# Turned w_up tiles of a hybrid decoder layer: one started per pair of row tiles in ScalarE's order, written whole to a place of their own two pairs later

## The chip, the cores and the metric

The kernel runs on one core of a Trainium2 chip. The metric is device microseconds of one execution, the median over several; lower is better. A core has TensorE (PE, matmuls into PSUM banks), VectorE (DVE), ScalarE (ACT), GpSimd (POOL) and SyncE (SP, which here issues nearly all DMAs). Each engine works through its own queue in order and waits at the head of it until what the instruction needs is there.

## The reference, cut to what matters

One decoder layer on 256 tokens of width 2048, all in float32. The change touches the last third, the MLP:

```python
def squared_relu_mlp(u, w_up, w_down):        # u 256 x 2048, w_up 2048 x 8192, w_down 8192 x 2048
    hdn = jax.nn.relu(jnp.einsum('bsd,df->bsf', u, w_up))
    return jnp.einsum('bsf,fd->bsd', hdn * hdn, w_down)

h = h + rmsnorm(mix, norm_mix_post)
h = h + rmsnorm(squared_relu_mlp(rmsnorm(h, norm_mlp_pre), w_up, w_down), norm_mlp_post)
```

## The kernel before

**Products.** Every weight tile (256 rows by 512 columns, 512 KB, two blocks of 128 rows) is fetched by SyncE into a place called `raw` and split in two fp32r parts: ScalarE writes `hi`, a rounded copy, and VectorE writes `lo` = raw - hi (`split`, L148 and L149). TensorE then forms a product from three matmuls: hi and lo with the rounded activations, hi with their remainder. There are five buffers each of hi and lo (`BUFS`), so ScalarE can be at most five tiles ahead of TensorE. A *row tile* is one weight tile with both halves of the tokens: 12 matmuls. A *pair of row tiles* is the same 256 weight rows for two neighbouring column blocks: 24 matmuls.

**Sevens.** For some rows k a pair of row tiles is done as one step of Strassen's scheme (`seven`): seven products (21 matmuls) in place of eight, with sums of weights made by VectorE (`e`, `r`, L261) and sums of activations (`sums_of_acts`, L400 to L405). Half of the second weight tile then comes as a sum made by GpSimd in DRAM (`pair`). `plan` lists for each unit the order of the rows and which of them are sevens.

**Units.** `unit` computes 256 tokens by two column blocks (1024 columns) over all rows. It accumulates in eight PSUM banks, `acc` (four) and `more` (four). After the last seven, `combine` (`combine_new`, L450 to L454) empties the four banks of `more` on ScalarE and VectorE; after the last pair, `at_end` empties `acc`. The next unit swaps the two: its first pair of row tiles writes where `more` was. The MLP goes in two halves `hf` of 4096 features: the units of w_up for 8 column blocks (7 units in all are planned so), then two units of w_down over those 4096 features, then the same again.

**Turned tiles.** A unit of w_up leaves four tiles of 128 tokens by 512 features, in `room["shared"]` (tiles `hb` and `wpost`). w_down needs them with the features on the partitions. `up_end` (L1470) adds the last bank (L1475), applies Relu on ScalarE (L1476) with high priority, and queues `turned` (L1480) in `beside`: Square (L1483), the 16-bit halves of each word put apart by a ScalarE copy into a place of halves (L1484), a DMA transpose back into the tile (L1485, on SyncE's queue), and some steps later the halves put together by a second ScalarE copy (L1490) into the same place of halves, and a split into the activations of w_down. `pump_beside` moves the oldest of these works one step on: once per row tile in w_up (`pace` 1, `lag` 2), twice in w_down (2 and 3), twice per seven. `drain_beside` finishes them all before `combine`, and in the first unit of each w_down before its first seven (`more_beside_down`, `more_in_place`), since the places of halves lie in `ha`, which then becomes the place for sums of activations or for weights.

**What sets the order.** The instructions of `weights` and `seven` carry a very high priority and are chained in the order of the program (`split_in_line`, `add_in_line`); the rest is put between them by a list scheduler. Weight tiles go round a ring of places: four in `raw`, and those in `room["raw"]`, which stage by stage are tiles that nothing else uses then (`mw0`, `mw1`, `mw2`, `ha`, `uc`). SyncE's queue holds fetches and transposes in one order, and a fetch waits there until its place is free.

## Time and profile before

| | |
|---|---|
| runs, median (lowest to highest) | 1463.38 us (1462.07 to 1464.75) |
| the profiled execution, its own time | 1466.13 us |
| its span, first to last instruction | 1464.0 us |
| TensorE busy in the span | 1438.5 us, 98% |
| VectorE, ScalarE busy | 1297.8 us, 89%; 999.0 us, 68% |
| granted TensorE clock, mean | 0.993 |
| TensorE, VectorE, ScalarE busy from 840 to 1440 us | 582.77, 551.22, 433.01 us of 600 |

The MLP's part that the change touches begins at about 850 us (the first turned tile is copied apart at 853.3 us) and ends with the kernel. Busy TensorE time counts pipelined matmuls: in an undisturbed stretch one begins every 0.227 us and is listed with 0.39 us.

### The profile page before, as it was taken

How to read it: one execution, taken by the hardware profiler on the slowest of the kernel's cores; microseconds unless marked ns; L12 is line 12 of the kernel's file. 1: busy time of each engine (PE TensorE's matmuls, PEld its weight loads, DVE VectorE, ACT ScalarE, POOL GpSimd, SP SyncE). 2: the span in 40 equal slices, each digit the busy share in tenths (PEclk: the TensorE clock that was granted, in tenths of full speed). 3: DMA queues.
4: the chain of work that ended last, by engine and by line, in shares of the span. 5: the costliest groups of instructions: out<-in, count | busy, mean ns of one | idle time of the engine just before them, and what ended most of it. 6: DMA issues, size and time to landing. Idle time of an engine off the chain costs nothing.

```text
span 1464.0 us, 20242 instructions
## 1 busy us (share of the span) xinstructions
PE 1438.5 (98%) x6930; PEld 1204.8 (82%) x6930; DVE 1297.8 (89%) x1881; ACT 999.0 (68%) x1407; POOL 162.7 (11%) x244
## 2 busy tenths in 40 slices
PE   9999999999999999999999999989999999989998
PEld 8888888888888888888888888867888887768886
DVE  7788888988999788699989999879889999969998
ACT  7577669675666666566667689855565888876564
POOL 0201110121101000010100111001111011101000
PEclk9999999999999999999999999989999999999999
DMA  8967666756888657588877799688888999989854
GB/s 267 280 204 222 188 186 182 236 173 187 245 256 240 190 130 243 204 246 268 266 215 228 236 314 286 195 192 237 271 253 247 260 273 270 271 211 305 261 197 164
DMA packets 201926, 340.30 MB, mean 232 GB/s; under 512 B 45616, under 2 KB 48544, under 8 KB 201824
## 3 DMA queue, kind: packets, MB, share of 16 engines
q1 hardware_dynamic: 174304, 279.72, 61.3%
q0 software_dynamic: 19648, 45.63, 15.4%
q10 hardware_dynamic: 7872, 13.68, 2.8%
q8 instruction: 54, 0.88, 0.2%
q14 instruction: 48, 0.39, 0.1%
HBM read 327.39 MB, written 49.84 MB: 258 GB/s over the span
## 4 chain that ended last, share of the span: by engine, by line
PE 61%; DVE 7%; ACT 4%; DMA 3%; issue 2%; SPq 0%; ACTq 0%; DVEq 0%
PE acc L355 8%; PE acc L353 8%; PE acc L354 8%; PE acc L442 5%; PE acc L443 5%; PE acc L441 5%; PE acc L510 4%; DVE lo L149 4%; PE acc L513 2%; PE ps L443 2%; PE ps L442 2%; PE ps L441 2%; PE ps L353 2%; PE ps L354 2%; PE ps L355 2%
## 5 line engine op out<-in xcount | busy, mean ns | idle before, releaser
L149 DVE TENSOR_TENSOR lo<-raw,hi 128x1024 fp32r<-128x1024 f32 (+1 forms) x402 | 487.1, 1218 | 79.1 <-ACT hi L148 76.8
L148 ACT ACTIVATE hi<-raw 128x1024 fp32r<-128x1024 f32 (+1 forms) x402 | 419.0, 1049 | 191.9 <-PE acc L355 50.0
L510 PE MATMUL acc<-ua,hi 128*128 128x512 f32 x520 | 141.2, 400 | 0.0
L148 ACT ACTIVATE hi<-e 128x1024 fp32r<-128x1024 f32 x66 | 69.7, 1057 | 49.3 <-DVE e L261 45.3
L510 PEld LDWEIGHTS acc<-ua,hi 128*128 128x128 f32 x520 | 91.3, 189 | 14.0
L353 PE MATMUL acc<-hi,ua 128*128 128x512 f32 x228 | 90.0, 395 | 0.0
L149 DVE TENSOR_TENSOR lo<-e,hi 128x1024 fp32r<-128x1024 f32 x66 | 80.5, 1220 | 10.3 <-ACT hi L148 9.9
L354 PE MATMUL acc<-lo,ua 128*128 128x512 f32 x228 | 89.2, 391 | 0.0
L355 PE MATMUL acc<-hi,ua 128*128 128x512 f32 x228 | 89.0, 390 | 0.0
L353 PE MATMUL acc<-hi,sh 128*128 128x512 f32 x220 | 86.4, 393 | 0.0
L355 PE MATMUL acc<-hi,sl 128*128 128x512 f32 x220 | 85.7, 389 | 0.0
L354 PE MATMUL acc<-lo,sh 128*128 128x512 f32 x220 | 85.6, 389 | 0.0
L513 PEld LDWEIGHTS acc<-ua,lo 128*128 128x128 f32 x520 | 76.5, 189 | 8.9
L513 PE MATMUL acc<-ua,lo 128*128 128x256 f32 x520 | 78.8, 281 | 0.0
L442 PE MATMUL acc<-lo,ah 128*128 128x512 f32 x180 | 70.6, 392 | 1.8 <-DVE lo L149 1.7
L441 PE MATMUL acc<-hi,ah 128*128 128x512 f32 x180 | 70.2, 390 | 0.6 <-ACT hi L148 0.6
L443 PE MATMUL acc<-hi,al 128*128 128x512 f32 x180 | 70.1, 389 | 0.0
L510 PE MATMUL acc<-uc,hi 128*128 128x512 f32 x208 | 61.4, 405 | 0.0
L443 PE MATMUL acc<-hi,ua 128*128 128x512 f32 x137 | 53.3, 389 | 0.0
L442 PE MATMUL acc<-lo,ua 128*128 128x512 f32 x137 | 53.3, 389 | 0.0
L441 PE MATMUL acc<-hi,ua 128*128 128x512 f32 x137 | 53.0, 390 | 0.0
L355 PEld LDWEIGHTS acc<-hi,ua 128*128 128x128 f32 x228 | 42.8, 188 | 9.0
(566 smaller groups left out, 3714.4 us busy)
## 6 DMA issues: line engine op xcount, KB each, us to landing
raw<-in_w_in_dram SPq DMA_DIRECT2D x154, 512.0 KB, 4.4
raw<-in_w_up_dram SPq DMA_DIRECT2D x77, 512.0 KB, 4.8
raw<-in_w_down_dram SPq DMA_DIRECT2D x70, 512.0 KB, 5.7
raw<-in_w_out_dram SPq DMA_DIRECT2D x38, 512.0 KB, 5.0
raw<-pair SPq DMA_DIRECT2D x59, 256.0 KB, 4.5
pair<-in_w_up_dram POOLq DMA_DIRECT2D x56, 256.0 KB, 6.3
pair<-in_w_down_dram POOLq DMA_DIRECT2D x52, 256.0 KB, 6.5
pair<-in_w_in_dram POOLq DMA_DIRECT2D x42, 256.0 KB, 5.4
```

Of the source, the lines that this page charges most:

```text
L148: return (nc.scalar.activation(hi, src, AF.Copy), nc.vector.tensor_tensor(lo, src, hi.bitcast(F32), op=ALU.subtract))
L149: nc.vector.tensor_tensor(lo, src, hi.bitcast(F32), op=ALU.subtract))
L353: nc.tensor.matmul(dst[:, cs], a_h[:, r, ts], hi[:, j, cs], start=begin and j == 0, stop=False)
L354: nc.tensor.matmul(dst[:, cs], a_h[:, r, ts], lo[:, j, cs], start=False, stop=False)
L355: product[t] = nc.tensor.matmul(dst[:, cs], a_l[:, r, ts], hi[:, j, cs], start=False, stop=end and j == KB - 1)
L441: nc.tensor.matmul(dst, a_h, hi[:, j], start=own and first, stop=False)
L442: nc.tensor.matmul(dst, a_h, lo[:, j], start=False, stop=False)
L443: nc.tensor.matmul(dst, a_l, hi[:, j], start=False, stop=own and last)
L510: nc.tensor.matmul(acc[f], hi[:, j, f * P:(f + 1) * P], u(k0 + j), start=k0 + j == 0, stop=False, skip_group_check=True)
L513: nc.tensor.matmul(acc[f][:, 0], lo[:, j, f * P:(f + 1) * P], u(k0 + j)[:, 0], start=False, stop=k0 + j == NK - 1, skip_group_check=True)
```

## The change

Six things move together.

1. A tile is started by `pump_beside` once per row k (a pair of row tiles or a seven) from the third row on, and each start is tied into ScalarE's order right behind the newest split (`newest["act"]`). Relu moves from `up_end` into `turned`.
2. It is finished by `land_beside` at the end of the second row after that, tied in the same way.
3. The halves are put together into `whole`, a tile named `junk` of its own (one buffer), and not into the place of halves.
4. There are two places of halves, used in turn, in place of four: `mw1` in the first half of the MLP, a third of `ha` in the second.
5. So in the first half `ha` gives three places for weights (before: one) and `mw1` none; in the second half two (before: one). `beside_down` takes `ha` for sums at once, and the second half's w_down uses two thirds of `ha` for weights from its start; the rest follows as `then`, when the last tile has landed.
6. In the first unit of each w_down the rows are in another order: the first seven is the fourth row there, before the fifth, and the sevens then alternate with other rows.

```diff
-    def beside_up(raws, turn):
+    def beside_up(raws, turn, halves=None):
...
-        room["halves"] = [a[:, i].bitcast(U16) for i in range(2 * NT)]
-        room["raw"], room["turn"], room["acts"], room["chain"] = [*raws, a[:, 2 * NT:]], turn, act_u, True
-        room["pace"], room["lag"] = 1, 2
+        in_a = [a[:, k:k + KB] for k in range(0, 3 * KB, KB)]
+        halves = in_a.pop(0) if halves is None else halves
+        room["halves"] = deque(halves[:, i].bitcast(U16) for i in range(KB))
+        room["raw"], room["turn"], room["acts"], room["chain"] = [*raws, *in_a], turn, act_u, True
+        room["of_halves"], room["of_a"] = halves, in_a
...
+    def pump_beside():
+
+        if not beside:
+            return
+        work = beside.popleft()
+        with tc.issue_after(newest["act"].ins):
+            next(work)
+        flying.append([work, 0])
+
+    def land_beside(steps=2):
+
+        for one in flying:
+            one[1] += 1
+        if flying and flying[0][1] > steps:
+            with tc.issue_after(newest["act"].ins):
+                next(flying.popleft()[0], None)
+        if not (beside or flying) and "then" in room:
+            room.pop("then")()
...
-            plan(("down", 0), w_down, 0, (0, 1, 2, 3, 4, 5, 6, 7, 9, 8, 10, 11, 12, 13), (4, 6, 9, 10, 11, 13))
+            plan(("down", 0), w_down, 0, (0,1,2,4,3,6,5,9,7,10,8,11,12,13), (4,6,9,10,11,13))
...
         for i, (k, by_seven) in enumerate(order):
+            if i >= 2:
+                pump_beside()
...
-                pump_beside(2)
...
+            land_beside()
...
-                nc.scalar.activation(r, r, AF.Relu, scale=rmlp[:, t:t + 1])
-            beside.append(turned(t, 4 * fb, r, room["halves"][NT * b + t]))
+            beside.append(turned(t, 4 * fb, r))
...
+        nc.scalar.activation(r, r, AF.Relu, scale=rmlp[:, t:t + 1])
         nc.scalar.activation(r, r, AF.Square)
...
-        steps = 0
-        while steps < room["lag"]:
-            steps += 1
-            yield
-        nc.scalar.activation(halves.rearrange("p (n h) -> p h n", h=2), words.rearrange("p (h n) -> p h n", h=2), AF.Copy)
+        yield
+        whole = hp.tile([P, NB], F32, name="junk")
+        nc.scalar.activation(whole.bitcast(U16).rearrange("p (n h) -> p h n", h=2), words.rearrange("p (h n) -> p h n", h=2), AF.Copy)
...
-        split(d_h[:, i:i + 4, ts], d_l[:, i:i + 4, ts], halves.bitcast(F32).rearrange("p (f s) -> p f s", f=4))
+        split(d_h[:, i:i + 4, ts], d_l[:, i:i + 4, ts], whole.rearrange("p (f s) -> p f s", f=4))
...
     in_u = room["raw"]
-    room["chain"], room["pace"], room["lag"] = True, 2, 3
+    room["raw"] = [*in_u, *room["of_a"]]
+    room["chain"] = True
```

The new text is 18 lines longer in all, so a line has another number after the change: Relu, Square and the first copy stand in L1500 to L1502, the transpose in L1503, the second copy in L1506, `up_end`'s addition in L1491, and `combine_new` in L464 to L468.

**First place: ScalarE where the first half of the MLP passes from w_up to w_down.** `hi` from `ha`, `raw` and `mw2` are the splits of weight tiles, `hb` and `wpost` the tiles of the unit of w_up that has just ended, `ha` (before) and `mw1` (after) the places of halves. Before:

```order
L1476 ACTIVATE hb_7889<-hb_7889,rmlp_5921 128x512 x2
L1483 ACTIVATE hb_7889<-hb_7889 128x512 x2
L1476 ACTIVATE wpost_7890<-wpost_7890,rmlp_5921 128x512
L1476 ACTIVATE wpost_7891<-wpost_7891,rmlp_5921 128x512
L148 ACTIVATE hi_9193<-mw2_6211 128x1024
L1484 ACTIVATE ha_7892<-hb_7889 128x1024
L148 ACTIVATE hi_9214<-raw_9212 128x1024
L1484 ACTIVATE ha_7892<-hb_7889 128x1024
L148 ACTIVATE hi_9243<-raw_9241 128x1024
L1483 ACTIVATE wpost_7890<-wpost_7890 128x512
L1483 ACTIVATE wpost_7891<-wpost_7891 128x512
L1484 ACTIVATE ha_7892<-wpost_7890 128x1024
```

and now, from the second copy of the third tile of the unit before on:

```order
L1506 ACTIVATE junk_9055<-wpost_7890 128x2x512
L148 ACTIVATE hi_9110<-raw_9108 128x1024
L148 ACTIVATE hi_9128<-raw_9126 128x1024
L148 ACTIVATE hi_9146<-raw_9144 128x1024
L148 ACTIVATE ah0_4884<-junk_9055 128x4x128
L148 ACTIVATE hi_9164<-raw_9162 128x1024
L1500 ACTIVATE hb_7889<-hb_7889,rmlp_5921 128x512
L1501 ACTIVATE hb_7889<-hb_7889 128x512
L1502 ACTIVATE mw1_6210<-hb_7889 128x1024
L148 ACTIVATE hi_9193<-mw2_6211 128x1024
L148 ACTIVATE hi_9211<-raw_9209 128x1024
L1506 ACTIVATE junk_9059<-wpost_7891 128x2x512
```

The four Relus in a row are gone and one tile at a time stands between the splits; the second copies of the unit before (L1506) now stand behind the first splits of w_down (a Relu of the second tile, L1500, stands ahead of the last row).

**Second place: VectorE at the same point.** `acc_8016` is the fourth bank of `more`, which the second row tile of w_down writes next; `lo` from `raw` are the splits of w_down's first tiles. Before:

```order
L452 TENSOR_TENSOR hb_7889<-acc_8016,r_9057 128x512
L453 TENSOR_TENSOR wpost_7890<-acc_8014,r_9057 128x512
L1475 TENSOR_TENSOR hb_7889<-acc_8009,hb_7889 128x512
L454 TENSOR_TENSOR wpost_7891<-acc_8016,wpost_7890 128x512
L1475 TENSOR_TENSOR hb_7889<-acc_8011,hb_7889 128x512
L149 TENSOR_TENSOR lo_9138<-raw_9135,hi_9137 128x1024
```

and now:

```order
L149 TENSOR_TENSOR lo_9129<-raw_9126,hi_9128 128x1024
L149 TENSOR_TENSOR lo_9147<-raw_9144,hi_9146 128x1024
L149 TENSOR_TENSOR lo_9165<-raw_9162,hi_9164 128x1024
L415 TENSOR_TENSOR r_9185<-r_9184 128x256
L149 TENSOR_TENSOR lo_9194<-mw2_6211,hi_9193 128x1024
L416 TENSOR_TENSOR r_9185<-r_9184,r_9185 128x128
L149 TENSOR_TENSOR al0_4885<-junk_9055,ah0_4884 128x4x128
L417 TENSOR_TENSOR r_9185<-r_9184,r_9185 128x128
L149 TENSOR_TENSOR lo_9212<-raw_9209,hi_9211 128x1024
L468 TENSOR_TENSOR wpost_7891<-acc_8016,wpost_7890 128x512
```

The last instruction of `combine` (L454, now L468) writes `wpost_7891`, which L1506 reads; so it has moved behind that copy, behind six splits of w_down's tiles.

**Third place: SyncE where the second half passes to w_down.** `uc` and `ha` are places for weights, `hb` and `wpost` the tiles that are turned. Before:

```order
L162 DMA uc_12045<-in_w_down_dram 128x2x512
L157 DMA uc_12045<-pair4_93 128x512
L158 DMA uc_12045<-in_w_down_dram 128x512
L1485 DMA_TRANSPOSE hb_10525<-ha_10528 128x8x128 x2
L1485 DMA_TRANSPOSE wpost_10526<-ha_10528 128x8x128
L1485 DMA_TRANSPOSE wpost_10527<-ha_10528 128x8x128
L162 DMA ha_12216<-in_w_down_dram 128x2x512 x3
```

and now:

```order
L158 DMA raw_12378<-in_w_down_dram 128x512
L1503 DMA_TRANSPOSE hb_10533<-ha_10536 128x8x128 x2
L162 DMA uc_12047<-in_w_down_dram 128x2x512 x2
L1503 DMA_TRANSPOSE wpost_10534<-ha_10536 128x8x128
L162 DMA ha_10536<-in_w_down_dram 128x2x512
L157 DMA ha_10536<-pair2_91 128x512
```

Weight fetches into `ha` stood behind all four transposes; now two of its places are used before the first transpose is issued (a row `ha_10536<-in_w_down_dram` stands ahead of the rows shown, too), and the transposes stand one by one between fetches.

More of the change, by code (lines that the diff above doesn't have):

```diff
@@ L199, in beside_up @@
         a = hp.tile([P, 3 * KB, NB], F32, name="ha")
[L200 to L202 removed]
+        in_a = [a[:, k:k + KB] for k in range(0, 3 * KB, KB)]
[3 more added lines that the diff above has]
+        room["of_halves"], room["of_a"] = halves, in_a
         sums_of.clear()
     def beside_down():
[L207 to L210 removed]
+        a = hp.tile([P, 3 * KB, 2, S], F32R, name="ha")
+        room["sums"] = [a[:, k] for k in range(3 * KB)]
+        room["raw"], room["turn"], room["acts"], room["then"] = [mws[2]], 0, part, more_beside_down
         sums_of.clear()
     def more_beside_down():
[L215 to L216 removed]
         b = hp.tile([P, KB, 2, S], F32R, name="hb")
[L218 removed]
+        room["sums"] += [b[:, k] for k in range(KB)]
         room["sums"] += [hp.tile([P, 2, S], F32R, name="wpost", bufs=2) for _ in range(2)]
+        m = new_mw(1, F32R)
+        room["sums"] += [m[:, t].rearrange("p (b s) -> p b s", b=2) for t in range(NT)]
     def fetch_next(src, k0, c0, pair=None):
@@ L242, in hymba_layer @@
     behind = []
-    line = {}
+    line, newest = {}, {}
     @contextmanager
@@ L316, in weights @@
                     order.enter_context(tc.issue_after(behind.pop().ins))
-                split(hi, lo, raw)
+                newest["act"] = split(hi, lo, raw)[0]
         return hi, lo
@@ L332, in drain @@
             pump()
-    beside = deque()
-    def pump_beside(n=1):
-        for _ in range(n):
-            if beside:
-                work = beside.popleft()
-                if next(work, work) is not work:
-                    beside.append(work)
+    beside, flying = deque(), deque()
+    def pump_beside():
[13 more added lines that the diff above has]
+            room.pop("then")()
     def drain_beside():
-        while beside:
+        while beside or flying:
             pump_beside()
+            land_beside(0)
     def row_tile(dst, t, parts, k0, acts, begin, end, cs=slice(0, NB)):
@@ L377, in row_tiles @@
             pump(pumps)
-            pump_beside(room.get("pace", 1))
     def gemm_tokens(src, c0, acts, nk, lag=0, at_end=None, pumps=1):
@@ L1537, in hymba_layer @@
     in_u = room["raw"]
-    room["chain"], room["pace"], room["lag"] = True, 2, 3
+    room["raw"] = [*in_u, *room["of_a"]]
+    room["chain"] = True
     def more_in_place():
-        drain_beside()
-        a, b = hp.tile([P, 3 * KB, NB], F32, name="ha"), hp.tile([P, KB, 2, S], F32R, name="hb")
-        room["raw"] = [*in_u, *(a[:, k:k + KB] for k in range(0, 3 * KB, KB))]
+        b = hp.tile([P, KB, 2, S], F32R, name="hb")
         room["sums"] += [b[:, k] for k in range(KB)]
+        room["turn"] %= RAWS + len(room["raw"])
+        room["raw"].append(room["of_halves"])
         for n in range(2):
             load_wpost(norm_mlp_post, n)
+    room["then"] = more_in_place
     unit(w_downs[1], 0, orders[("down", 1), 0], (14, 15), acc, more,
-         lambda x: combine_onto(0, x), 0, (complete(0), complete(1)), ready=more_in_place)
+         lambda x: combine_onto(0, x), 0, (complete(0), complete(1)))
     room["chain"] = False
```

18 lines of the change are left out of this document (7 added, 11 removed).

## The prediction

> **What bounds the kernel now.** TensorE is busy for 98% of the span, and no matmul is added or removed, so a gain can only come from TensorE's own waits. I read first who waits for whom, TensorE alone, from 840 us on (total, times, longest).
>
> ```profile
> PE ps L353 <- ACT hi L148: 6.9, 1, 6.9
> PE acc L441 <- ACT hi L148: 6.7, 3, 5.4
> PE acc L442 <- DVE lo L149: 3.1, 6, 0.8
> PE ps L1433 <- ACT dg L1432: 1.4, 1, 1.4
> PE ps L354 <- DVE lo L149: 0.4, 2, 0.2
> ```
>
> Two waits hold most of it. L1433 is the kernel's end, which the change leaves alone. The timeline of TensorE (start, duration, in brackets the idle time before and who ended it) shows where the others lie and what follows them.
>
> ```profile
> 958.70 0.39 PE L441 MATMUL acc<-hi,mw 128*128 128x512 f32 x1
> 959.72 0.50 PE L442 MATMUL acc<-lo,mw 128*128 128x512 f32 x1 [0.63 <-DVE lo L149]
> 966.51 0.80 PE L441 MATMUL acc<-hi,mw 128*128 128x512 f32 x1 [5.36 <-ACT hi L148]
> 967.77 0.80 PE L442 MATMUL acc<-lo,mw 128*128 128x512 f32 x1 [0.46 <-DVE lo L149]
> 972.74 0.40 PE L355 MATMUL ps<-hi,sl 128*128 128x512 f32 x1
> ...
> 1202.72 0.50 PE L442 MATMUL acc<-lo,ah 128*128 128x512 f32 x1 [0.49 <-DVE lo L149]
> 1244.77 0.50 PE L441 MATMUL acc<-hi,ah 128*128 128x512 f32 x1 [0.64 <-ACT hi L148]
> 1246.03 0.50 PE L442 MATMUL acc<-lo,ah 128*128 128x512 f32 x1 [0.76 <-DVE lo L149]
> 1275.07 0.39 PE L353 MATMUL acc<-hi,uc 128*128 128x512 f32 x1
> 1280.51 0.39 PE L353 MATMUL ps<-hi,sh 128*128 128x512 f32 x1
> 1306.90 0.39 PE L443 MATMUL ps<-hi,sl 128*128 128x512 f32 x1
> 1314.16 1.22 PE L353 MATMUL ps<-hi,sh 128*128 128x512 f32 x2 [6.87 <-ACT hi L148]
> 1318.05 0.40 PE L353 MATMUL ps<-hi,sh 128*128 128x512 f32 x1
> ```
>
> From 1275.07 to 1280.51 stand the 24 matmuls of one pair of row tiles: 0.227 us each. At the first passage from w_up to w_down, 958.70 to 972.74, 17 matmuls take 14.04 us in place of 3.86: 10.2 us lost, of which some 3 are slow matmuls (0.63 to 0.80 us) after the long wait. At the second, 1306.90 to 1318.05, 11 matmuls take 11.15 in place of 2.50: 8.6 us. The other waits are 6.7 - 5.4 + 3.1 - 0.63 - 0.46 + 0.4 - 0.2 = 3.5 us, 1.9 of them in the second w_up (the rows at 1202 to 1246). **In all 22.3 us can go.**
>
> Next, who made the two long waits: ScalarE's and SyncE's timelines.
>
> ```profile
> 942.61 1.04 ACT L1484 ACTIVATE ha<-hb 128x1024 uint16<-128x1024 uint16 x1
> 956.13 1.37 ACT L1490 ACTIVATE ha<-hb 128x1024 uint16<-128x1024 uint16 x1 [4.29 <-DMA hb<-ha]
> 964.21 1.34 ACT L1490 ACTIVATE ha<-wpost 128x1024 uint16<-128x1024 uint16 x1 [4.05 <-DMA wpost<-ha]
> 965.43 1.03 ACT L148 ACTIVATE hi<-mw 128x1024 fp32r<-128x1024 f32 x1
> 1303.94 1.36 ACT L1490 ACTIVATE ha<-wpost 128x1024 uint16<-128x1024 uint16 x1
> 1313.05 1.06 ACT L148 ACTIVATE hi<-ha 128x1024 fp32r<-128x1024 f32 x1 [6.75 <-DMA ha<-in_w_down_dram]
> ```
>
> ```profile
> 945.88 2.27 SPq L162 DMA_DIRECT2D raw<-in_w_down_dram  x2
> 948.21 6.74 SPq L1485 DMA_TRANSPOSE hb<-ha  x2
> 958.22 5.00 SPq L1485 DMA_TRANSPOSE wpost<-ha  x1
> 1307.13 1.41 SPq L162 DMA_DIRECT2D ha<-in_w_down_dram  x3
> ```
>
> First passage: the first tile's halves are ready at 943.65, its transpose leaves SyncE only at 948.21 behind fetches, and the second copies (L1490) wait at the head of ScalarE, with the split at 965.43, for which TensorE waits, behind them. Second passage: the next places for weights are in `ha`, which holds halves until the last L1490 at 1303.94 and its split are through; the fetch leaves at 1307.13 and lands at 1313.
>
> **The change, step by step.** Per turned tile (28 of them) ScalarE still does Relu, Square, two copies and a split, SyncE one transpose, VectorE one split: nothing added, nothing saved. `whole` costs what L1490 does, being the same shape. The first passage's long wait needs an L1490 whose transpose is late; now each tile is landed two rows after its start, where some 12 to 15 us of other ScalarE work lie between, and transposes land as follows (group, count, median to landing, 920 to 960 us):
>
> ```profile
> raw<-in_w_down_dram SPq DMA_DIRECT2D x11, 512.0 KB, 5.4
> mw<-in_w_down_dram SPq DMA_DIRECT2D x1, 512.0 KB, 8.4
> hb<-ha SPq DMA_TRANSPOSE x2, 7.5
> wpost<-ha SPq DMA_TRANSPOSE x2, 8.3
> ```
>
> So that wait goes; if SyncE holds a transpose 5 us (958.22), cover is still there. The second long wait goes too: two thirds of `ha` hold no halves, and the fetches into them stand ahead of the first transpose. That transpose stands behind many fetches and is about 7 us late for its L1506, but TensorE then has five buffered tiles, some 7 us, in hand; I cost it at nothing, and at its 4 us of waiting (964.21) if the cover were gone.
>
> **What is late next** is the last instruction of `combine`, L454, now L468. It frees the fourth bank of `more`, overwrites `wpost_7891`, and now has to wait for L1506 of the unit before, which stands behind w_down's first splits on ScalarE; VectorE's queue stands behind it, and TensorE needs the bank. The rows for it:
>
> ```profile
> 1275.24 0.68 DVE L451 TENSOR_TENSOR r<-hb,ps 128x512 f32<-128x512 f32 x1
> 1278.77 0.68 DVE L454 TENSOR_TENSOR wpost<-acc,wpost 128x512 f32<-128x512 f32 x1
> ...
> L149 DVE TENSOR_TENSOR lo<-raw,hi 128x1024 fp32r<-128x1024 f32 x155 | 187.8, 1220 | 12.9 <-ACT hi L148 12.2
> L148 ACT ACTIVATE hi<-raw 128x1024 fp32r<-128x1024 f32 x155 | 162.0, 1053 | 62.3 <-PE acc L355 21.2 <-DMA raw<-in_w_down_dram 21.0 <-DMA raw<-in_w_up_dram 9.2
> L1490 ACT ACTIVATE ha<-wpost 128x1024 uint16<-128x1024 uint16 x14 | 19.0, 1358 | 4.4 <-DMA wpost<-ha 4.4
> ```
>
> Count from the last pair of w_up (0 = 1275.07 at the second passage). Before, VectorE begins `combine` at 0.2 and ends L454 at 4.4. TensorE comes to the bank at 5.4 + 18 x 0.227 = 9.5; the new order puts 11 matmuls (first passage) or 5 (second) of the next tile ahead: 12.0 and 10.6.
> - First passage. VectorE frees the place of w_down's first tile after five additions of 0.6 and a `lo`: 4.3. The fetch into it takes 5.4, then come a split 1.05, a Relu 0.6, L1506 1.36: 12.7, L468 ends 13.4. TensorE waits 1.4 us. By a landing of 8.4 it is 4.4; by VectorE's own row of work alone L468 ends at 12.9 and by ScalarE's buffers at 11.9, so nothing is the other end.
> - Second passage. 4.3 + 5.4 + 1.05 + 1.36 = 12.1, another 0.1 behind VectorE's own work, L468 ends 12.9: TensorE waits 2.2 us, by a landing of 8.4 5.2, by buffers alone nothing.
> - Three passages from unit to unit inside w_up: L468 stands behind eight additions, three `lo` and one L1506, and ends at 9.1 with the bank due at 9.5. I take 0.3 us each, 0.9, between 0 and 1.2 each (a transpose held 5 us).
>
> The waits in w_up (1.9 us) I let go: they follow clumps of Relus that are spread now, and a ring of five places that has six. Of the others 1.4 us stay, because VectorE is full there (busy us by engine in two stretches after the passages):
>
> ```profile
> 970.00:1020.00 50.00, 48.78 (x204) 38.16 (x203) 49.50 (x67) 31.92 (x37) 5.45 (x8) 0.97 0.79 227
> 1320.00:1370.00 50.00, 49.31 (x218) 40.40 (x217) 49.96 (x70) 32.19 (x37) 6.78 (x10) 1.00 0.92 282
> ```
>
> The third busy time is VectorE's: 49.5 and 49.96 of 50 us. The order of rows moves a seven earlier there and changes no sum; the alternation keeps VectorE's work even. I cost it at nothing, between -1 and 3 us.
>
> **Sum.** Left are 1.4 + 2.2 + 0.9 + 1.4 = 5.9 us of 22.3: 16.4 us gained. The profiled execution took 1466.13 us, so 1449.7; that one is 2.75 us above the runs' median, so against them **1447 us**.
>
> Whether such a wait also slows the matmuls behind it, the rows show from both sides: 0.76 us did not (0.50 us, then the usual pace), 5.36 us did, for some 3 us lost. My waits lie between, nearer the short one, so I add nothing. [...]
>
> **Rivals.**
> - *The bank waits take their far end.* For: landings of 8.4 us are in the trace, and L468 depends on one at both passages. Against: the median is 5.4. Then 4.4 + 5.2 with 3 us of slow matmuls each, 15.6 in place of 3.6: 1459 us.
> - *VectorE becomes the bound.* For: the stretches above. Its work between 920 and 1020 us must now fit in 10 us less, and every wait at L468 idles it. Against: the long ScalarE waits idled it before. Another 2 to 3 us at each passage: 1452 us.
> - *It doesn't do what it says*: second copies still wait at ScalarE's head, at 4 us for each of two late transposes at both passages, 16 us back: 1463 us. Against: the cover of 12 us.
> - *Slower.* One `junk` and L468 tie transpose, ScalarE, VectorE and bank in a ring at five passages. If the fourth tile's transpose lands later than about 12 us after its copy, L468 ends after 9.5 at each of them. At 5 us and 3 us of slow matmuls: 5 x 8 = 40 us in place of 4.5: 1482 us. Against: 8.3 us is the landing seen.
>
> **How the numbers follow.** Forecast 0.55 (1442 to 1452), far bank waits 0.18, VectorE 0.13, not as said 0.06, slower 0.08. A measurement of this kernel tells some 0.2%, 3 us, from no change. Faster: the first three, 0.86; same 0.06; slower 0.08. The range goes from 1439, all 22.3 us gone and the short matmul gaps behind each wait with them, to 1460, the far bank waits.
>
> **What would show it.** Right: no idle time before the second copies (L1506) that passes to TensorE, no `ha` wait of 6.75 us, and TensorE's longest wait after 850 us a matmul on the fourth bank of `more`, released by VectorE's L468, at 1 to 5 us, twice. Wrong: waits of that kind at the passages inside w_up, a clock below full there, or L1506 waiting for transposes longer than 4 us.

## The result and the profile after

| | before | changed |
|---|---|---|
| runs, median (lowest to highest) | 1462.72 us (1460.11 to 1464.75) | 1447.99 us (1446.84 to 1449.47) |
| the profiled execution's span | 1464.0 us | 1446.6 us |
| granted TensorE clock, mean | 0.993 | 0.999 |

The ratio is 0.9901 (95% interval 0.9882 to 0.992): 1% faster, 14.7 us between these medians and 17.4 us between the two profiled spans (the profiled execution of the kernel before took 1466.13 us, 3.4 us more than the median here). The forecast was 1447.0 us.

Who waits for whom in the changed kernel, TensorE alone, from 840 us on (total, times, longest):

```profile
PE acc L368 <- DVE wpost L468: 3.4, 3, 2.0
PE ps L1449 <- ACT dg L1448: 1.4, 1, 1.4
PE ps L369 <- DVE lo L149: 1.2, 2, 0.7
PE acc L456 <- DVE lo L149: 0.9, 2, 0.7
```

Without the kernel's end (L1449) 5.5 us of waits are left, of 17.1 before. Both long ones on ScalarE are gone, and the largest is now the fourth bank of `more`, released by VectorE's L468. TensorE's timeline says where:

```profile
943.42 0.50 PE L368 MATMUL acc<-hi,sh 128*128 128x512 f32 x1 [1.05 <-DVE wpost L468]
1189.72 0.50 PE L368 MATMUL acc<-hi,ua 128*128 128x512 f32 x1 [0.38 <-DVE wpost L468]
1275.55 0.50 PE L368 MATMUL acc<-hi,sh 128*128 128x512 f32 x1 [1.99 <-DVE wpost L468]
```

1.05 us at the first passage, 0.38 inside w_up, 1.99 at the second passage. ScalarE and VectorE at the first passage show how L468 comes to be late:

```profile
929.47 1.36 ACT L1506 ACTIVATE junk<-wpost 128x1024 uint16<-128x1024 uint16 x1
941.27 1.37 ACT L1506 ACTIVATE junk<-wpost 128x1024 uint16<-128x1024 uint16 x1 [0.99 <-DVE al L149]
```

```profile
935.48 3.48 DVE L149 TENSOR_TENSOR lo<-raw,hi 128x1024 fp32r<-128x1024 f32 x3
938.88 0.41 DVE L415 TENSOR_TENSOR r<-r 128x256 f32<-128x256 f32 x1
939.22 1.21 DVE L149 TENSOR_TENSOR lo<-mw,hi 128x1024 fp32r<-128x1024 f32 x1
940.35 0.28 DVE L416 TENSOR_TENSOR r<-r 128x128 f32<-128x128 f32 x1
940.56 0.68 DVE L149 TENSOR_TENSOR al<-junk,ah 128x512 fp32r<-128x512 f32 x1
941.16 0.28 DVE L417 TENSOR_TENSOR r<-r 128x128 f32<-128x128 f32 x1
941.36 1.21 DVE L149 TENSOR_TENSOR lo<-raw,hi 128x1024 fp32r<-128x1024 f32 x1
942.67 0.69 DVE L468 TENSOR_TENSOR wpost<-acc,wpost 128x512 f32<-128x512 f32 x1
```

The last tile's second copy (941.27) waits for the one buffer of `junk`, which VectorE empties at 940.56, in the middle of a row of work without a pause. No fetch is waited for. At the second passage one is:

```profile
1265.81 1.06 ACT L148 ACTIVATE hi<-raw 128x1024 fp32r<-128x1024 f32 x1 [1.50 <-DMA raw<-in_w_down_dram]
...
1267.76 1.06 ACT L148 ACTIVATE hi<-raw 128x1024 fp32r<-128x1024 f32 x1 [0.37 <-DMA raw<-in_w_down_dram]
1269.06 1.06 ACT L148 ACTIVATE hi<-raw 128x1024 fp32r<-128x1024 f32 x1 [0.23 <-DMA raw<-in_w_down_dram]
1270.03 0.71 ACT L1500 ACTIVATE hb<-hb,rmlp 128x512 f32<-128x512 f32 x1
...
1272.39 1.04 ACT L148 ACTIVATE hi<-raw 128x1024 fp32r<-128x1024 f32 x1
1273.34 1.33 ACT L1506 ACTIVATE junk<-wpost 128x1024 uint16<-128x1024 uint16 x1
```

After the three waits for fetches, 2.1 us in all, ScalarE has no pause: Relu (1270.03), Square and first copy of the next tile, a split, and then L1506.

Where the time went is best seen by stages. As marks I take the start of the third instruction of `combine` (L452 before, L466 now) in VectorE's timeline. Those of the first unit of w_down, before and now:

```profile
931.22 0.68 DVE L452 TENSOR_TENSOR hb<-acc,r 128x512 f32<-128x512 f32 x1
1021.20 0.68 DVE L452 TENSOR_TENSOR mw<-acc,r 128x512 f32<-128x512 f32 x1
```

```profile
931.95 0.68 DVE L466 TENSOR_TENSOR hb<-acc,r 128x512 f32<-128x512 f32 x1
1010.89 0.68 DVE L466 TENSOR_TENSOR mw<-acc,r 128x512 f32<-128x512 f32 x1
```

| stage, us between marks | before | changed |
|---|---|---|
| w_up, first half (three units) | 81.8 | 82.9 |
| **first passage**, first unit of w_down | 90.0 | 78.9 |
| second unit of w_down | 77.5 | 75.9 |
| w_up, second half | 178.2 | 177.7 |
| **second passage** to the end of the span | 187.0 | 182.1 |

Two thirds of the gain lie behind the first passage, most of the rest behind the second; w_up itself gains about 1 us at most. One profile gives a stage to 1 or 2 us: the kernel called "`ha` late" below, which changes nothing ahead of the second half's w_down, has 84.1 us in the first stage. And the marks are VectorE's: in the kernels of this document they stand between 0.1 us ahead of TensorE's first matmul behind the last seven and 2.7 us after it. By these matmuls of TensorE (1275.07 before and 1262.75 now at the second passage) the second unit of w_down takes 76.8 us before and now, so its 1.6 us are not a gain; the first passage goes from 90.2 to 78.9 us and the second from 188.9 to 183.9. Last, the busy times in the first 40 us after each passage's mark, before and now (the third busy time is VectorE's):

```profile
931.20:971.20 40.00, 33.55 (x138) 26.65 (x137) 25.11 (x36) 27.32 (x34) 2.72 (x4) 0.89 0.86 209
1277.00:1317.00 40.00, 33.09 (x140) 26.37 (x139) 27.06 (x38) 29.34 (x36) 1.36 (x2) 0.92 0.82 220
```

```profile
932.00:972.00 40.00, 38.95 (x172) 31.94 (x171) 37.81 (x54) 34.63 (x42) 4.07 (x6) 1.00 0.92 242
1264.50:1304.50 40.00, 37.51 (x165) 30.40 (x164) 34.28 (x48) 32.47 (x39) 4.07 (x6) 1.00 0.99 282
```

VectorE did 25.1 and 27.1 us of work in these 40 us and now does 37.8 and 34.3. This will turn out to carry more than the single waits.

### The profile page after: what moved, and what is told of

Read it like the earlier page. It is cut to its first block, busy times and chain, and to the rows that moved or that the text cites. A ratio compares the mean times of both kernels' runs of the same rounds, so it can differ in the third digit from the quotient of the medians.

```text
span 1446.6 us, 20277 instructions
## 1 busy us (share of the span) xinstructions
PE 1432.3 (99%) x6930; PEld 1201.5 (83%) x6930; DVE 1297.6 (90%) x1881; ACT 1000.4 (69%) x1407; POOL 162.6 (11%) x244
## 5 line engine op out<-in xcount | busy, mean ns | idle before, releaser
L149 DVE TENSOR_TENSOR lo<-raw,hi 128x1024 fp32r<-128x1024 f32 (+1 forms) x390 | 472.6, 1217 | 82.8 <-ACT hi L148 80.6
L148 ACT ACTIVATE hi<-raw 128x1024 fp32r<-128x1024 f32 (+1 forms) x390 | 406.2, 1048 | 170.2 <-PE acc L370 49.1
L368 PE MATMUL acc<-hi,ua 128*128 128x512 f32 x228 | 90.4, 396 | 0.4 <-DVE wpost L468 0.4
L370 PE MATMUL acc<-hi,ua 128*128 128x512 f32 x228 | 89.1, 391 | 0.0
L149 DVE TENSOR_TENSOR lo<-ha,hi 128x1024 fp32r<-128x1024 f32 x48 | 58.3, 1218 | 3.0 <-ACT hi L148 2.7
L148 ACT ACTIVATE hi<-ha 128x1024 fp32r<-128x1024 f32 x48 | 50.2, 1050 | 6.9 <-PE acc L370 2.0
L455 PE MATMUL acc<-hi,ua 128*128 128x512 f32 x137 | 53.5, 391 | 0.0
```

The source lines that it names most:

```text
L148: return (nc.scalar.activation(hi, src, AF.Copy), nc.vector.tensor_tensor(lo, src, hi.bitcast(F32), op=ALU.subtract))
L149: nc.vector.tensor_tensor(lo, src, hi.bitcast(F32), op=ALU.subtract))
L368: nc.tensor.matmul(dst[:, cs], a_h[:, r, ts], hi[:, j, cs], start=begin and j == 0, stop=False)
L370: product[t] = nc.tensor.matmul(dst[:, cs], a_l[:, r, ts], hi[:, j, cs], start=False, stop=end and j == KB - 1)
L455: nc.tensor.matmul(dst, a_h, hi[:, j], start=own and first, stop=False)
```

## The experiments

Twelve kernels, each timed against the kernel before on the same chip, whose median there was 1462.3 to 1463.6 us. Unless said otherwise each is the changed kernel with one edit. S1 and S2 are the stages behind the first and the second passage by VectorE's marks as above, V1 and V2 VectorE's busy time in the first 40 us of each. They come from one profiled execution of each kernel; those of "no tie" and "sevens a row earlier still" were 4.5 and 3.1 us longer than the median.

| edit | median, us (lowest to highest) | ratio to before, 95% | V1 | S1 | V2 | S2 |
|---|---|---|---|---|---|---|
| kernel before | 1462.7 | | 25.1 | 90.0 | 27.1 | 187.0 |
| the change | 1448.0 (1446.8 to 1449.5) | 0.9882 to 0.992 | 37.8 | 78.9 | 34.3 | 182.1 |
| old order of rows | 1456.5 (1453.4 to 1457.0) | 0.993 to 0.9973 | 36.1 | 79.1 | 28.8 | 189.1 |
| kernel before, new order | 1462.1 (1458.5 to 1467.6) | 0.9975 to 1.0008 | 32.1 | 84.6 | 27.1 | 188.8 |
| `ha` late | 1449.9 (1449.2 to 1451.2) | 0.9891 to 0.9932 | 37.1 | 79.7 | 35.0 | 181.5 |
| finished in the same row | 1462.4 (1459.9 to 1468.5) | 0.9982 to 1.0015 | 38.0 | 78.7 | 33.5 | 184.3 |
| finished one row later | 1459.8 (1455.3 to 1462.8) | 0.9951 to 0.9981 | 38.1 | 79.3 | 35.0 | 182.5 |
| all finished before the first seven | 1451.6 (1449.8 to 1453.8) | 0.9897 to 0.9942 | 37.4 | 79.3 | 35.1 | 182.1 |
| that, and old places | 1451.3 (1449.6 to 1455.5) | 0.9891 to 0.9938 | 34.9 | 81.7 | 34.4 | 182.7 |
| Relus together | 1458.9 (1456.1 to 1462.3) | 0.9941 to 0.9976 | 38.0 | 79.2 | 34.0 | 182.8 |
| no tie | 1454.0 (1451.3 to 1458.5) | 0.9906 to 0.9958 | 33.1 | 83.5 | 33.5 | 183.1 |
| L468 into another tile | 1456.7 (1454.2 to 1458.2) | 0.9943 to 0.9975 | 38.2 | 78.9 | 34.4 | 183.0 |
| sevens a row earlier still | 1449.9 (1449.3 to 1453.0) | 0.9879 to 0.992 | 37.8 | 79.0 | 35.7 | 182.6 |
| start a row earlier | 1445.5 (1444.9 to 1446.1) | 0.9858 to 0.9907 | 37.3 | 78.9 | 33.7 | 184.1 |

Differences of 1 or 2 us in S1 and S2 can be the marks'. By TensorE's own marks S1 and S2 are 80.5 and 191.1 us with the old order of rows, 84.8 and 191.3 in the kernel before with the new order, 82.9 and 183.4 without ties, and 77.7 and 184.4 with the start a row earlier; the second unit of w_down is 76.8 us in every kernel.

### The order of rows, undone and alone

```diff
-            plan(("down", 0), w_down, 0, (0,1,2,4,3,6,5,9,7,10,8,11,12,13), (4,6,9,10,11,13))
+            plan(("down", 0), w_down, 0, (0, 1, 2, 3, 4, 5, 6, 7, 9, 8, 10, 11, 12, 13), (4, 6, 9, 10, 11, 13))
-    plan(("down", 1), w_downs[1], 0, (0, 1, 2, 3, 4, 6, 5, 8, 7, 9, 10, 11, 12, 13), (3, 6, 8, 9, 11, 13))
+    plan(("down", 1), w_downs[1], 0, (0, 1, 2, 4, 3, 5, 6, 7, 8, 10, 9, 12, 11, 13), (3, 6, 8, 9, 11, 13))
```

> Undone alone: the order of rows in the first unit of each w_down; all else as in the changed kernel (1448.0 us). Theory (the prediction): the order only decides how many matmuls of the next tile stand ahead of the fourth bank of more, so the waits at that bank stay within about 1 us of 1.0 and 2.0 us, no wait of 5 us or more comes back, and the time is 1446 to 1451 us. Rival (the gain came from the order of rows, since the first seven now stands where the turned tiles are through): most of the 14.7 us comes back, 1455 us or more, with a wait above 4 us on ScalarE's hi or VectorE's lo at one of the two passages.

Measured 1456.5 us, 8.5 more than the change: the theory falls, though no wait as the rival had it came back. S1 hardly moves (at most 1.6 us, by TensorE's marks); S2 is 189.1 us, longer even than before the change. The second passage in that run, VectorE's waits in the first 40 us, and TensorE:

```profile
DVE lo L149 <- ACT hi L148: 11.1, 9, 3.8
```

```profile
1278.46 0.80 PE L368 MATMUL acc<-hi,sh 128*128 128x512 f32 x1 [3.85 <-DVE wpost L468]
1279.05 0.63 PE L369 MATMUL acc<-lo,sh 128*128 128x512 f32 x1
1279.48 0.63 PE L370 MATMUL acc<-hi,sl 128*128 128x512 f32 x1
```

The bank wait is 3.85 us in place of 1.99, and the matmuls behind it are slow (0.43 us from start to start, not 0.227; the granted clock is 0.96 in the 40 us from 1265.8, where it is 1.00 in the changed kernel's 40). VectorE, with the first seven a row later, idles 11.2 us in that stretch (11.1 of them for `hi`), where it idles 5.7 in the changed kernel, and is full afterwards: busy 39.9 of the next 40 us.

Then the kernel before with the new order alone (the same edit the other way round).

> The kernel before with one part of the change alone: the new order of rows in the first unit of each w_down. Theory (order and late finishing only work together: the first seven, ahead of which the kernel before finishes all turned tiles, now comes a row earlier, when the transposes are later still; what VectorE gains by an early seven is lost in that wait): within 3 us of before or slower, 1460 to 1472 us. Rival (the order gives its 8.5 us by itself, since VectorE gets the sevens' sums while it has time): 1452 to 1456 us.

Measured 1462.1 us against 1463.6 for the kernel before on the same chip: nothing that can be told. The order gives 5.4 us at the first passage (S1 84.6) and takes 1.8 at the second, where the old wait for a place is still there. ScalarE and SyncE:

```profile
1298.43 1.35 ACT L1490 ACTIVATE ha<-wpost 128x1024 uint16<-128x1024 uint16 x1
...
1305.89 1.06 ACT L148 ACTIVATE hi<-ha 128x1024 fp32r<-128x1024 f32 x1 [5.45 <-DMA ha<-in_w_down_dram]
```

```profile
1301.20 0.37 SPq L162 DMA_DIRECT2D ha<-in_w_down_dram  x1
```

The fetch leaves at 1301.20, after the last second copy and its split, as the prediction read it. So at the second passage neither part gains anything alone (189.1 and 188.8 against 187.0), and together they gain 4.9 us.

### Where the second passage's places are

```diff
-    room["raw"] = [*in_u, *room["of_a"]]
...
-        room["raw"].append(room["of_halves"])
+        room["raw"] += [*room["of_a"], room["of_halves"]]
```

> In the second half's w_down no part of ha is a place for weights until the last tile has landed (places of the ring there: two fewer, 6 in place of 8, until then); all else as in the changed kernel. Theory (the prediction's reason for the second passage: fetches wait for places that hold halves, so the two free thirds of ha are what took away the 8.6 us): TensorE waits again between 1280 and 1310 us, 3 to 8 us, and the time is 1451 to 1456 us. Rival (places were never short there; it was the landing of all four tiles ahead of the first seven, with the fetches behind it, that cost them, and 6 places of 5.4 us landing serve a tile each 2.7 us): no new wait above 1 us, 1447 to 1450 us.

1449.9 us, S2 181.5, no new wait above 0.8 us: the rival. The two thirds of `ha` aren't needed early; this kernel adds them once the last tile is through. What is left as the reason is that no fetch comes to a place that still holds halves. That is argued, not tested by a run of its own.

### When a tile is finished

Three edits: in the row of its start, one row later, or all ahead of the first seven.

```diff
-    def land_beside(steps=2):
+    def land_beside(steps=0):
```

> A turned tile is finished at the end of the row in which it is started, not two rows later; all else as in the changed kernel. Theory (the prediction: the first long wait is a second copy at ScalarE's head whose transpose is late, and the two rows of other work are the cover): second copies wait for transposes 3 to 6 us each, at the two passages that reaches TensorE, 5 to 10 us at each, and the time is 1458 to 1475 us; inside w_up the five buffers hide most of it. Rival (the tie to the newest split, the places and the spread Relus took the wait away, the lag is only margin): no wait above 2 us comes back, 1446 to 1450 us, and with the copies earlier the 3.4 us at the fourth bank go.

1462.4 us, the whole gain lost, within the theory's numbers but not where it said: S1 is 78.7 us. The loss is in w_up (89.0 and 183.7 us, against 82.9 and 177.7) and 2.2 us behind the second passage. ScalarE's second copies in that run, from 840 us on (busy, mean, idle time before them and who ended it):

```profile
L1506 ACT ACTIVATE junk<-hb 128x1024 uint16<-128x1024 uint16 x14 | 19.1, 1366 | 12.8 <-DMA hb<-ha 7.8 <-DMA hb<-mw 4.7 <-DVE al L149 0.2
```

That is the wait for late transposes. The changed kernel has it nowhere; here all of it stands in the units of w_up, none at the passages.

```diff
-    def land_beside(steps=2):
+    def land_beside(steps=1):
```

> Turned tiles are finished one row after the start in place of two; all else as in the changed kernel. Theory (the 3.4 us at the fourth bank come from a second copy that stands too late, and one row, 5.4 us, is as much cover as a transpose of 5.7 us needs): those waits shrink to under 1 us, no other grows, 1444 to 1447 us. Rival (finishing in the row of the start gave 1462.4 us, and one row is still too little cover where SyncE holds a transpose): second copies wait for transposes 1 to 3 us each, a third to two thirds of that loss comes back, 1451 to 1457 us.

1459.8 us: the rival, a little beyond its numbers. Second copies wait 13.0 us for transposes in all, w_up is 3.9 and 5.8 us longer, S1 and S2 stay. One row is too little cover.

```diff
-                 lambda x: combine_new(in_mw(0), x), 0, (onto(0), onto(1)))
+                 lambda x: combine_new(in_mw(0), x), 0, (onto(0), onto(1)), ready=drain_beside)
...
-         lambda x: combine_onto(0, x), 0, (complete(0), complete(1)))
+         lambda x: combine_onto(0, x), 0, (complete(0), complete(1)), ready=drain_beside)
```

> As the changed kernel, but in the first unit of each w_down all turned tiles are finished ahead of the first seven, as it was before the change; two of the four are started and finished there one behind the other. Theory (the first long wait came from second copies that are forced ahead of a seven's splits while their transposes are late; the two rows of lag are what takes it away): second copies wait 3 to 6 us for transposes at ScalarE's head at both passages, 5 to 10 us of it reach TensorE at each, 1458 to 1470 us, and the stage from the first passage to the end of the first unit of w_down, 78.9 us now and 90.0 before, is 84 to 90. Rival (the places of halves and weights and the new order of rows gave the gain, the finishing can stand anywhere): 1447 to 1451 us and that stage 78 to 80.

1451.6 us, S1 79.3, S2 182.1. The rival, but for 0.6 us. Finishing all four tiles ahead of the first seven does no harm at the passages.

### The old places of the first half

On top of the last edit:

```diff
-        beside_up([*tiles_of(mws[0], (0, NB)), mws[2]], -2 * RAWS, mws[1])
+        beside_up([*tiles_of(mws[0], (0, NB)), mws[1], mws[2]], -2 * RAWS)
...
-        a = hp.tile([P, 3 * KB, 2, S], F32R, name="ha")
-        room["sums"] = [a[:, k] for k in range(3 * KB)]
+        m = new_mw(1, F32R)
+        room["sums"] = [m[:, t].rearrange("p (b s) -> p b s", b=2) for t in range(NT)]
```

> As the run with all turned tiles finished ahead of the first seven (1451.6 us), and in the first half also the places of the kernel before: halves in a third of ha (two places, in turn), mw1 a place for weights in its stead, and the sums of w_down's first seven in mw1, those of the later ones in ha once the last tile is through. Theory (what took the first passage from 90.0 us to 78.9 is that the sums no longer wait for the halves in ha): the stage comes back to 84 to 90 us, 1457 to 1463 us. Rival (it is when the tiles are started: one per row, tied behind the newest split, so that four transposes no longer stand together in SyncE's queue; where the halves lie is nothing): 78 to 80 us for the stage, 1450 to 1453 us.

1451.3 us, as without it; S1 81.7, some 2 us longer, with one wait of 0.76 us. The theory falls: these places alone aren't what took 11 us off the first passage.

### How a tile is started

```diff
-        with tc.issue_after(newest["act"].ins):
-            next(work)
+        next(work)
...
-            with tc.issue_after(newest["act"].ins):
-                next(flying.popleft()[0], None)
+            next(flying.popleft()[0], None)
```

> As the changed kernel, but starts and second copies are not tied behind the newest split; the scheduler puts them where it finds room (it puts the four tiles of a unit close together, the Relus of hb and wpost two by two). Theory (starting one tile per row in ScalarE's real order is what keeps clumps and late transposes away): waits of 1 to 5 us come back in w_up as in the run with the Relus together (1458.9 us) and the second copies wait for transposes, 1455 to 1463 us. Rival (the tie decides little, since the program starts one tile per row anyway): 1447 to 1450 us.

1454.0 us: below the theory's numbers, above the rival's. It is the edit of the machinery that lengthens S1 most, to 83.5 us, and w_up's first half is 86.7; but the execution that shows this was the slowest of the four, so how much of it is typical stays open. S1 has one cluster of waits: a first copy waits 4.6 us for its place at 959.60 us, and TensorE then 1.9 and 0.8 us from 962.7 us on.

```diff
-            beside.append(turned(t, 4 * fb, r))
+                nc.scalar.activation(r, r, AF.Relu, scale=rmlp[:, t:t + 1])
+            beside.append(turned(t, 4 * fb, r))
...
-        nc.scalar.activation(r, r, AF.Relu, scale=rmlp[:, t:t + 1])
```

> Undone alone: Relu is again done in the step that adds the last bank, four together with high priority, and not when a tile is started. Theory (the prediction: the short waits of the second w_up, 1.9 us before and 0.7 + 0.4 now, follow clumps of Relus): waits of 0.5 to 0.8 us come back behind the clumps in w_up, 1 to 3 us in all, and at the first passage the four Relus, 2.5 us, stand ahead of the first splits and delay L468 by 1 to 2 us; 1449 to 1453 us. Rival (ScalarE has 5 tiles in hand in w_up and hides it): within 1 us of the changed kernel, 1447 to 1449 us.

1458.9 us, more than the theory had; waits on `hi` of 1.1 to 1.3 us came back in w_up as it said, S1 didn't move. Both edits let tiles start closer together, and the price shows in the groups of ScalarE's first copies (L1502; two line numbers lower, L1500, in the kernel without ties), in this order: the change, Relus together, no tie:

```profile
L1502 ACT ACTIVATE ha<-wpost 128x1024 uint16<-128x1024 uint16 x8 | 8.4, 1055 | 5.2 <-DMA hb<-ha 5.1
L1502 ACT ACTIVATE mw<-wpost 128x1024 uint16<-128x1024 uint16 x6 | 6.3, 1053 | 0.9 <-DMA hb<-mw 0.8
```

```profile
L1502 ACT ACTIVATE ha<-wpost 128x1024 uint16<-128x1024 uint16 x8 | 8.4, 1056 | 13.5 <-DMA hb<-ha 13.4
L1502 ACT ACTIVATE mw<-wpost 128x1024 uint16<-128x1024 uint16 x6 | 6.3, 1055 | 6.5 <-DMA hb<-mw 6.5
```

```profile
L1500 ACT ACTIVATE ha<-wpost 128x1024 uint16<-128x1024 uint16 x8 | 8.4, 1051 | 6.7 <-DMA hb<-ha 6.6
L1500 ACT ACTIVATE mw<-wpost 128x1024 uint16<-128x1024 uint16 x6 | 6.3, 1052 | 10.3 <-DMA hb<-mw 10.2
```

With two places of halves the third tile's first copy can't begin until the first tile's transpose has read its place. That costs ScalarE 5.9 us in the changed kernel, 19.9 and 16.8 here. So two places serve as long as the starts stand far apart. No run gave the two kernels more places, so how much of their loss is this wait isn't shown.

### The wait that is left

```diff
+            s = room["fourth"] if b and t else r
-            nc.vector.tensor_tensor(r, acc, r, op=ALU.subtract if b else ALU.add)
+            nc.vector.tensor_tensor(r, acc, s, op=ALU.subtract if b else ALU.add)
...
+    def combine_up(more):
+        room["fourth"] = tmp()
+        hb, (wp0, _) = room["shared"]
+        combine_new((hb, (wp0, room["fourth"])), more)
```

> The last addition of combine in w_up (L468) writes a tile of r in place of wpost, and the addition of the last bank reads it there; so nothing of L468 waits for the second copy of the unit before. All else as in the changed kernel. Theory: the three waits at the fourth bank of more (3.4 us in all, 1.0 at 943 us, 0.4 in w_up, 2.0 at 1275 us) go, since they come from that write alone; time 1443.5 to 1446 us. Rival 1 (VectorE is full there and TensorE only waits for it somewhere else): the same 3.4 us stand as waits on lo, 1447 to 1449 us. Rival 2 (the addition behind it, which now waits for the copy, holds VectorE's queue as L468 did): waits on lo or on a bank of 1 to 3 us at the same places, 1446 to 1450 us.

1456.7 us, 8.7 us worse, and none of the three. L468 waits for nothing any more, but the scheduler ordered everything about it anew. The instruction ahead of it, L467, writes the third tile and now waits as L468 did (2.5 us at the second passage). And in w_up, the first copy (L1503 in this kernel) waits for its place, which passes to TensorE, here from ScalarE's timeline and TensorE's:

```profile
919.66 1.06 ACT L1503 ACTIVATE mw<-wpost 128x1024 uint16<-128x1024 uint16 x1 [3.59 <-DMA hb<-mw]
```

```profile
921.72 0.49 PE L455 MATMUL acc<-hi,ah 128*128 128x512 f32 x1 [2.30 <-ACT hi L148]
```

Next, more of what the order gave: sevens a row earlier again in the second half.

```diff
-    plan(("down", 1), w_downs[1], 0, (0, 1, 2, 3, 4, 6, 5, 8, 7, 9, 10, 11, 12, 13), (3, 6, 8, 9, 11, 13))
+    plan(("down", 1), w_downs[1], 0, (0, 1, 3, 2, 6, 4, 8, 5, 9, 7, 11, 10, 12, 13), (3, 6, 8, 9, 11, 13))
```

> As the changed kernel, with the sevens of the first unit of the second half's w_down one row earlier still: the first is the third row there, then every second row, the plain rows last. Theory (VectorE is the limit of that unit, and what it does not do in the first 40 us it owes at the end: idle 5.4 us of the 40 in the changed kernel, 11.2 with the old order, and that cost 7.0 us): idle falls by 2 to 4 us, the stage from the second passage to the end from 182.1 to 179 to 181 us, 1444.5 to 1447 us. Rival (the early seven's sums now stand ahead of L468 in VectorE's queue, or its two tiles of weights land too late): the wait at the fourth bank grows from 2.0 to 4 us or more, with slow matmuls behind it, 1450 to 1456 us.

1449.9 us: no gain, and just short of the rival's numbers. VectorE did 1.5 us more in its 40 us, and the bank wait grew from 2.0 to 3.35 us: what the one gained the other about lost.

Last, every start a row earlier, with the same lag:

```diff
-            if i >= 2:
+            if i >= 1:
                 pump_beside()
```

> As the changed kernel, but the first tile of a unit is started in the second row of the next unit, not in the third, so all starts and second copies stand a row earlier with the same lag of two rows. In VectorE's order L468 then follows the sums of combine directly at the first passage, and stands behind the splits of w_down at the second as it does now. Theory (the 1.0 us at the first passage and the 2.0 us at the second come from a last second copy that stands behind w_down's first splits): no wait at the fourth bank at the first passage, the one at the second stays at 1 to 2.5 us; 1445.5 to 1448 us. Rival (the clumps of ScalarE work now meet the sevens of w_up, as they did where tiles were finished early): waits on hi of 1 to 3 us come back in w_up, 1450 to 1458 us.

1445.5 us (ratio to the kernel before 0.9882, interval 0.9858 to 0.9907). Its four runs (1444.9 to 1446.1) lie below all of the changed kernel's, but the two intervals overlap and the chips differ, so that it is faster than the changed kernel by some 2 us is likely and not proven. TensorE's waits from 840 us on, and ScalarE's second copies of `wpost`:

```profile
PE acc L368 <- DVE wpost L468: 3.0, 1, 3.0
PE ps L1449 <- ACT dg L1448: 1.4, 1, 1.4
```

```profile
L1506 ACT ACTIVATE junk<-wpost 128x1024 uint16<-128x1024 uint16 x14 | 19.2, 1370 | 6.5 <-DVE al L149 4.6 <-DVE sl L149 1.3 <-DMA raw<-in_w_up_dram 0.6
```

No wait at the first passage, as the theory said, none in w_up, and the first copies wait 0.4 us in all, in place of 5.9. The wait at the second passage grew to 3.0 us, above the theory's 2.5. By TensorE's marks the first passage is 1.2 us shorter than in the changed kernel, the second w_up 2.8 us shorter and the second passage 0.6 us longer. So most of the gain lies in w_up, of which the theory said nothing.

## Why the prediction was right, and where its reasons were not

**The sum.** It let 22.3 us go and put 5.9 back. What is left is 5.5: 1.05 us at the first passage (forecast 1.4), 1.99 at the second (2.2), 0.38 inside w_up (0.9), 2.1 behind VectorE's `lo` (1.4). The spans differ by 17.4 us where 16.4 was forecast.

**The new wait.** Place, instruction and size were right. L468 ended 12.7 us after the start of the last pair at the second passage (1262.75 in TensorE's timeline; forecast 12.9). ScalarE waits for w_down's fetches there, but these waits end after 6.3 us, where the sum let the fetch land at 9.7; the Relu, Square and first copy of the next tile (2.4 us) and a further split fill the time between. At the first passage it ended after 13.2 us (930.19; forecast 13.4), but by another way: the sum went by a fetch, and the trace shows VectorE's own row of work (12.9 in the prediction) and the one buffer of `junk`. So that both sums came within 0.2 us is in part luck. So is that 1.99 us cost no more than itself, as the last section shows.

**The step that failed: "The order of rows ... changes no sum ... I cost it at nothing, between -1 and 3 us."** Undone alone it costs 8.5 us; added alone to the kernel before it gives nothing that can be told, so its worth depends on the rest. VectorE is full in the stretches that were quoted, so what it leaves undone before them is late at their end. A seven that comes a row earlier gives it that work while it would idle. The sum stayed right since it let TensorE's waits go, whatever took them away, and the new order, priced at nothing, was part of what did. In that, too, there is luck.

**The reason for the first passage was too narrow: "now each tile is landed two rows after its start".** The wait went, but three edits of that lag leave S1 at 78.7 to 79.3 us. The lag is needed in w_up, which the prediction hardly looked at: without it w_up loses 6 us in each half. At the first passage no single part carries the 11.1 us. Undoing the tie gives back 4.6 in the one profile there is, the old places some 2, the order 0.2 (1.6 by TensorE's marks), the lag and the Relus nothing; the order alone, on the kernel before, brings 5.4. The parts stand in for one another. Which of the rest (starts once per row, `whole` in its own buffer) does how much stays open: the old way of starting on the new places, and `whole` in the place of halves, weren't tried.

**The reason for the second passage was half right.** Before the change ScalarE did wait for a fetch into a place that had held halves, as in the run of the kernel before with the new order again (5.45 us). But "two thirds of `ha` hold no halves" isn't the cure, since the kernel that uses them late has no such wait and is as fast behind that passage.

**What ties the runs together.** Across all fourteen kernels V1 + S1 lies between 115.1 and 117.4 us, while S1 goes from 78.7 to 90.0: with each microsecond that VectorE idles in the first 40 us the stage is about a microsecond longer, because VectorE is full in the rest of it (busy 49.8 of the last 50 us before, 38.8 of the last 38.9 now). V2 + S2 is less even, 214.1 to 218.3 us for S2 from 181.5 to 189.1. That is a relation of the runs, carried by the four of them whose V1 is low, and it doesn't say what made VectorE idle: often it was the same wait that TensorE had.

**The rivals.** Neither bank wait took its far end. The ring by `junk` is there: second copies of `wpost` idled ScalarE 13.1 us for VectorE's splits in the changed kernel. But only 3.4 us of that passed to TensorE. What the prediction had no rival for is the number of places of halves, for which ScalarE waits 17 to 20 us once the starts move closer.

## What to carry to other kernels

When TensorE waits for a late helper, look at what the second busiest engine could have done meanwhile: here the first unit of w_down was as long as VectorE's work in it and what VectorE idled at its start, and the order of rows, as a part of this change, was worth 8.5 us. A buffer count is only right for a spacing of its users, so price edits that move starts (a tie, an early Relu, a priority) together with the buffers. And a dependency that is taken away under a scheduler can reorder its neighbours: that cost 8.7 us here, while starting the tiles a row earlier took away the same wait at the first passage and cost nothing in all.

## What the runs showed of the hardware

The matmuls behind a wait of TensorE were slow in some cases and not in others, and not by the length of the wait alone. TensorE behind a wait of 2.83 us (finished one row later), behind one of 3.35 us (sevens a row earlier still), and behind waits of 1.94 and 0.76 us, which end at 964.62 and 965.88 (no tie):

```profile
1171.27 0.79 PE L455 MATMUL ps<-hi,ua 128*128 128x512 f32 x1 [2.83 <-ACT hi L148]
1172.53 0.80 PE L456 MATMUL ps<-lo,ua 128*128 128x512 f32 x1 [0.47 <-DVE lo L149]
1173.12 0.63 PE L457 MATMUL ps<-hi,ua 128*128 128x512 f32 x1
1173.55 0.63 PE L455 MATMUL acc<-hi,ua 128*128 128x512 f32 x1
```

```profile
1281.82 0.50 PE L368 MATMUL acc<-hi,sh 128*128 128x512 f32 x1 [3.35 <-DVE wpost L468]
1282.16 0.40 PE L369 MATMUL acc<-lo,sh 128*128 128x512 f32 x1
1282.39 0.39 PE L370 MATMUL acc<-hi,sl 128*128 128x512 f32 x1
```

```profile
966.22 0.39 PE L368 MATMUL ps<-hi,sl 128*128 128x512 f32 x1
...
966.91 0.47 PE L368 MATMUL ps<-hi,sl 128*128 128x512 f32 x1
967.18 0.63 PE L366 MATMUL ps<-hi,sh 128*128 128x512 f32 x1
```

The first, with a second wait of 0.47 us right behind it, is followed by matmuls 0.43 us apart, some 3 us lost until 1177.4; the second by the usual 0.23 (granted clock 1.00 in the 40 us from 1268.6). In the third case the usual pace holds for 1.3 us behind the waits, and only then do matmuls stand 0.43 us apart, until 970.55: the granted clock is 1.00 from 966 to 967 us and 0.57 from 967 to 971. Behind the one wait of 3.03 us with the start a row earlier, which ends at 1272.91, it is the same: 1.3 us at the usual pace, then matmuls 0.43 us apart until 1277.57, some 1.6 us lost. A fixed limit by the length of one gap doesn't fit these cases: matmuls were slow behind 1.94 and 0.76 us and behind 3.03 us, and not behind 3.35 us. No run moved a gap on purpose, so what decides it is not shown. For a sum this means that the 1.99 us here cost no more than itself (0.34 us to the next matmul, then the usual 0.23, clock 1.00 from 1275.5 to 1290), and that waits of 2 to 4 us did or did not cost more: nothing behind the 3.35 us, but behind the 3.85 us of the run with the old order seven matmuls lost some 1.5 us.
